# Rotating start places for the two parts of each weight chunk in a float32r decoder trunk

## The chip, the cores and the metric

The kernel runs on one core of one Trainium2 chip. The metric is the device time of one execution in microseconds (us). TensorE is called PE here, its loads of the stationary operand PEld, VectorE DVE, ScalarE ACT, GpSimd POOL and SyncE SP.

## The reference

Two residual layers over 256 tokens of 2048 features, float32, and one final norm. The first layer mixes tokens with a gated MLP, the second with an attention that forgets; each is followed by a feed-forward part with a short causal convolution. Cut to its products:

```python
def chunked_gmlp(xn, w_in, v_norm, w_s, b_s, w_out):
    z = jax.nn.gelu(xn @ w_in, approximate=False)          # 2048 -> 4096
...
    return gated @ w_out                                   # 2048 -> 2048

def conv_ffn(xn, w_up, conv_w, conv_b, w_down):
    h = xn @ w_up                                          # 2048 -> 11264
...
    return (jax.nn.silu(gate) * val) @ w_down              # 5632 -> 2048
...
for l in range(DEPTH):
    if l < N_A:
        h = h + chunked_gmlp(rmsnorm(h, a_norm[l]), ...)
    else:
        h = h + forgetting_attention(rmsnorm(h, b_norm[j]), w_qg, ..., k_sh, v_sh, c_sh)
    h = h + conv_ffn(rmsnorm(h, f_norm[l]), f_w_up[l], ...)
    if l == N_A - 1:
        k_sh, v_sh, c_sh = fox_shared_kv(h, kv_norm, w_kvf, b_f, k_norm)
return rmsnorm(h, final_norm)
```

Nearly all of the arithmetic is the products with the big weight matrices. Every weight is used once.

## The kernel before

All weights flow through one stream of 786 chunks (class `Stream`). A chunk is 128 partitions of up to 1024 float32 values. For each chunk three steps are issued: `_load` brings it from memory into `raw` (by SP's DMA queue, six chunks ahead), `_split` makes two parts of it (three chunks ahead), and `mult` multiplies. The split is one ACT instruction (L82), which writes `whi`, the weight rounded to the matmul's float32r format, and one DVE instruction (L83), which writes `wlo`, the rest that the rounding left. `raw`, `whi` and `wlo` have four buffers each, which are used in turn.

The activations are held in two parts too, side by side: columns 0 to 255 of a feature tile are the rounded part, columns 256 to 511 its rest. They lie in `X1` (shown as X), `mlp_X`, `att_X` or `ffn_H`, by the stage.

There are two forms of product, and in them the weight parts play opposite roles:

- `feat_block` (656 chunks: both FFNs, the MLP's u and output, the gate and the attention's output). The weights are stationary, and PE loads 128x128 pieces of `whi` and `wlo` in turn. For each piece of `whi` it streams 512 columns of activations past, and for the piece of `wlo` 256 columns (only the rounded part). A chunk is eight such pairs of matmuls. The last product of a block, and that alone, has the two the other way round.
- `tok_block` (128 chunks: the MLP's v, the attention's q, k and v). The activations are stationary, and 512 columns of `whi`, `wlo` and again `whi` stream past: twelve matmuls of 512 columns to a chunk. The blocks for the MLP's v and for q use X, those for k and v use att_X.

One more chunk makes the forget gates, with 16 columns of weights at a time. Sums stay in PSUM for a block's whole length; then ACT and DVE take them out while PE goes on with the next block's `ps` buffer (there are three).

The order of the instructions on each engine is that in which the program is written, since the schedule is manual. Where a tile lies in a partition's memory follows from the order and size of the pools: constants with `X1`, then the pool of `raw`, `whi` and `wlo`, then small tiles, then the phase's own tiles (`mlp_X`, `att_X`, `ffn_H` and the rest). Each tile begins on a multiple of 32 bytes. In the built program all eight buffers of `whi` and `wlo` begin 32 bytes past a multiple of 64, and so does `X1` (byte 36,192); `mlp_X`, `att_X` and `ffn_H` begin at byte 129,152, which is a multiple of 64. Inside a tile, every operand of a product begins a multiple of 512 bytes from the tile's start (64 bytes in the forget chunk).

Of the kernel before, what the change touches and what calls it, by code (L numbers as in the profile page):

```python
# [10 lines left out]
F32 = mybir.dt.float32  # L11
F32R = mybir.dt.float32r
# [5 lines left out]
P = 128  # L18
# [4 lines left out]
KF = FFN // P  # L23
NH = 16
CHUNK = 1024
EPS = 1e-6
SCALE = 128 ** -0.5
AHEAD = 3
LOADS = 6
NEG = -3e38  # L30

# Columns of the packed per-partition constants.
C_ANORM, C_KVNORM, C_BNORM, C_FNORM, C_FINAL, C_AVNORM = 0, 16, 32, 48, 80, 96
C_KNORM, C_QNORM, C_BF = 112, 113, 114
C_CONVW = 115
# [2 lines left out]


class Stream:  # L40
    """Weights that stream past: each chunk is loaded, split into two exact parts and multiplied."""

    def __init__(self, nc, pool):
        self.nc, self.pool = nc, pool
# [28 lines left out]
    def _split(self, i):  # L73
        if self.items[i][3]:
            self.items[i][3]()
        raw = self.raw.pop(i, None)
        if raw is None:
            return
        n = raw.shape[1]
        hi = self.pool.tile([P, CHUNK], F32R, name="whi", tag="whi")  # L80
        lo = self.pool.tile([P, CHUNK], F32R, name="wlo", tag="wlo")
        self.nc.scalar.activation(hi[:, :n], raw, AF.Copy)  # L82
        self.nc.vector.tensor_tensor(lo[:, :n], raw, hi[:, :n].bitcast(F32), op=OP.subtract)  # L83
        self.parts[i] = (hi, lo)
# [18 lines left out]


class Phase:
    """Tiles that live as long as one phase; the memory passes to the next phase."""

    def __init__(self, tc):
        self.tc, self.ctx, self.pool, self.name = tc, None, None, None
# [23 lines left out]
def build(ctx, tc, d, out):  # L133
# [26 lines left out]
    def column(i):  # L160
        return col[:, i:i + 1]

    # ------------------------------------------------------------ products
    def mm(o, a, b, start, stop):
        nc.tensor.matmul(o, a, b, start=start, stop=stop, skip_group_check=True)  # L165

    def feat_block(src, x, K, done):
        """[256 features, tokens], weights stationary; the result is the sum of both halves of columns."""
        box = {}
        n = K // 4  # L170
        for c in range(n):
            def mult(hi, lo, c=c):
                if c == 0:
                    box["ps"] = main_ps()
                ps, xx = box["ps"], x()
                for j in range(4):
                    kt = 4 * c + j
                    for m in range(2):
                        w = slice(j * 256 + m * P, j * 256 + (m + 1) * P)
                        if kt < K - 1:  # L180
                            mm(ps[:, m, :], hi[:, w], xx[:, kt, :], kt == 0, False)
                            mm(ps[:, m, :T], lo[:, w], xx[:, kt, :T], False, False)
                        else:
                            mm(ps[:, m, :T], lo[:, w], xx[:, kt, :T], False, False)
                            mm(ps[:, m, :], hi[:, w], xx[:, kt, :], False, True)
                if c == n - 1:
                    s.start(done(ps))
            s.chunk(src[c], mult)

    def tok_block(src, x, done, load=None, prep=None):  # L190
        """[tokens, 512 features], activations stationary; load(c), prep(c): what comes ahead of chunk c."""
        box = {}
        cuts = [(c, 0, 2) for c in range(8)]
        if prep:
            cuts[:1] = [(0, 0, 1), (0, 1, 1)]
        for c, j0, nj in cuts:
            def mult(hi, lo, c=c, j0=j0, nj=nj):
                kt0 = 2 * c + j0
                if kt0 == 0:
                    box["ps"] = main_ps()  # L200
                ps, xx = box["ps"], x()
                for j in range(nj):
                    kt = kt0 + j
                    w = slice(j * 512, (j + 1) * 512)
                    for tb in range(2):
                        a = xx[:, kt, tb * P:(tb + 1) * P]
                        b = xx[:, kt, T + tb * P:T + (tb + 1) * P]
                        mm(ps[:, tb, :], a, hi[:, w], kt == 0, False)
                        mm(ps[:, tb, :], a, lo[:, w], False, False)
                        mm(ps[:, tb, :], b, hi[:, w], False, kt == KD - 1)  # L210
                if kt0 + nj == KD:
                    s.start(done(ps))
            s.chunk(src[c][:, j0 * 512:(j0 + nj) * 512], mult,
                    load and c and (lambda c=c: load(c)), prep and c and (lambda c=c: prep(c)))

    # ------------------------------------------------------------ helpers
    def prep(dst, kt, gain):
        """dst[kt] = the two parts of h[kt] * gain."""
        g = column(gain + kt)
        nc.scalar.activation(dst[:, kt, :T], h[:, kt, :], AF.Copy, scale=g)  # L220
        nc.vector.scalar_tensor_tensor(dst[:, kt, T:], h[:, kt, :], g, dst[:, kt, :T].bitcast(F32),  # L221
                                       op0=OP.mult, op1=OP.subtract)
# [3 lines left out]
        nc.vector.tensor_tensor(dst[..., T:], src, dst[..., :T].bitcast(F32), op=OP.subtract)  # L226

    def rsqrt(y, v, n):
        """y = v ** -0.5: a guess from halving the exponent, then Newton's steps."""
        t = small.tile([P, n], F32, name="rs_t", tag=f"rs_t{n}", bufs=2)  # L230
        nc.vector.tensor_scalar(y.bitcast(I32), v.bitcast(I32), -0.5, 1597463007.0, op0=OP.mult, op1=OP.add)
        for _ in range(3):
            nc.vector.scalar_tensor_tensor(t, y, -0.5, y, op0=OP.mult, op1=OP.mult)
            nc.vector.tensor_tensor(t, t, v, op=OP.mult)
            nc.vector.scalar_tensor_tensor(y, t, 1.5, y, op0=OP.add, op1=OP.mult)

    def token_sums(rest=None):
        """rcol = (sum over features of acc, and rest, / D + eps) ** -0.5."""
        mp = misc_ps()
        parts = [acc] + ([] if rest is None else [rest[:, 0, :], rest[:, 1, :]])  # L240
        for tb in range(2):
            for i, a in enumerate(parts):
                nc.tensor.matmul(mp[:, tb:tb + 1], a[:, tb * P:(tb + 1) * P], ones[:, :1],  # L243
                                 start=i == 0, stop=i == len(parts) - 1)
        v = small.tile([P, 2], F32, name="ts_v", tag="ts_v", bufs=2)
        nc.vector.tensor_scalar(v, mp[:, :2], 1.0 / D, EPS, op0=OP.mult, op1=OP.add)
        rsqrt(rcol, v, 2)

    def token_rows():
        """rcol's values along the columns, the same on every partition."""  # L250
        mp = misc_ps()
        for tb in range(2):
            nc.tensor.transpose(mp[:, tb * P:(tb + 1) * P], rcol[:, tb:tb + 1].to_broadcast([P, P]), ident)
        return mp
# [15 lines left out]
                eng.tensor_tensor(acc, acc, sq[:, i, :], op=OP.add)  # L270

    def scaled_sum(ps, a):
        """a = (ps[.., :T] + ps[.., T:]) * rB."""
        t = small.tile([P, 2, T], F32, name="half", tag="half", bufs=2)
        nc.scalar.activation(t, ps[:, :, T:], AF.Copy)  # L275
        nc.vector.tensor_tensor(a, ps[:, :, :T], t, op=OP.add)  # L276
        nc.vector.tensor_tensor(a, a, rB[:, None, :].to_broadcast([P, 2, T]), op=OP.mult)  # L277

    def residual(p, gain):
        """Add a pair of feature tiles to h; then the next norm's operand and sum of squares."""  # L280
        def done(ps):
            hh = h[:, 2 * p:2 * p + 2, :]
            nc.vector.tensor_tensor(hh, hh, ps[:, :, :T], op=OP.add)
# [7 lines left out]
        return done  # L291

    def final(p, gain):
        """As residual, but the norm's result is the output."""
        def done(ps):
            kts = (2 * p, 2 * p + 1)
            sq = small.tile([P, 2, T], F32, name="sq", tag="sq", bufs=2)
# [18 lines left out]
            yield  # L316
        return done

    # ------------------------------------------------------------ input
    def load_input(c):  # L320
        nc.sync.dma_start(h[:, 2 * c:2 * c + 2, :], d["xT"][:, 2 * c:2 * c + 2, :])

# [13 lines left out]
        yield  # L336
        nc.scalar.activation(rB, token_rows()[:, :T], AF.Copy)

    # ------------------------------------------------------------ gated MLP
    def mlp_kept():  # L340
        ph.open("mlp")
        return (ph.keep("X2", [P, KD, 2 * T], F32R), ph.keep("vt", [P, 2, D]), ph.keep("wT", [P, NH, P]),
# [55 lines left out]
            two_parts(X2[:, 2 * p:2 * p + 2, :], u)  # L398
        return done

    # ------------------------------------------------------------ convolved FFN
    def ffn_h():
        ph.open(f"ffn{state['layer']}")
        return ph.keep("H", [P, KF, 2 * T], F32R)
# [28 lines left out]
        for p in range(8):  # L433
            feat_block(d[f"down{l}"][11 * p:11 * p + 11], ffn_h, KF, done(p))

    # ------------------------------------------------------------ attention
    def att(key):
        ph.open("att")
        shape = {"X2": [P, KD, 2 * T], "q": [P, NH, T], "k": [P, NH, T], "v": [P, 2, D],
# [8 lines left out]
            yield  # L448

    def head_norm(key, blk, gain):  # L450
        """q or k of four heads: normed per head, then features on the partitions."""
        def done(ps):
            dst = att(key)
            for tb in range(2):
# [44 lines left out]
        s.start(forget_sums(ps))  # L499

    def forget_sums(ps):
        """c = cumulative sum of log sigmoid(f), log1p as 2 atanh(y / (2 + y)) in its series."""
        t = [ph.temp("big", [P, 512], bufs=6) for _ in range(2)]
        z, m, y, q = (t[i][:NH, j * T:(j + 1) * T] for i in range(2) for j in range(2))
        nc.scalar.activation(z, ps[:NH, 0, T:], AF.Copy)
# [77 lines left out]
        state["done"] += 1  # L583

    def heads():
        """Starts a head at every second step."""
        n = 0
        while n < NH:
            if state["heads"]:
# [17 lines left out]
            state["gates"] += 1  # L607
        return done

    # ------------------------------------------------------------ the stream  # L610
    state = {"layer": 0, "heads": [], "done": 0, "gates": 0}
    cd = dram.tile([NH, T], F32, name="cd")

    nc.scalar.dma_start(col[:, :C_KVNORM], d["col"][:, :C_KVNORM])
    load_input(0)
    nc.gpsimd.memset(ones, 1.0)
    warm = small.tile([P, 2], F32, name="warm")
    nc.scalar.activation(warm, ones, AF.Gelu)
    nc.gpsimd.memset(ident, 1.0)
    nc.gpsimd.affine_select(ident, ident, pattern=[[-1, P]], compare_op=OP.is_equal, fill=0.0,  # L620
                            base=0, channel_multiplier=1)
# [31 lines left out]


def feat_chunks(w, order=None):
    """[K, N] -> chunks [N / 256 * K / 512, 128, 4 * 256]; order: the 128-wide tiles of the columns."""
    K, N = w.shape
    a = w.reshape(K // 512, 4, P, N // P, P)
    if order is not None:
# [3 lines left out]


def tok_chunks(w):
    """[K, N] -> chunks [N / 512 * K / 256, 128, 2 * 512]."""
    K, N = w.shape
    a = w.reshape(K // 256, 2, P, N // 512, 512)
    return np.ascontiguousarray(a.transpose(3, 0, 2, 1, 4)).reshape(-1, P, CHUNK)
# [43 lines left out]
```

## Time and profile before

| what | value |
|---|---|
| median of 3 runs | 2284.31 us (2284.15 to 2284.43) |
| span of the profiled execution, first to last instruction | 2282.4 us |
| outside that span (median less span) | 1.9 us |
| PE busy, share of the span | 99% |
| mean granted TensorE clock | 0.997 |
| memory traffic | 184 GB/s over the span |

The profiled execution is known by its span. The runs were timed without a profile, and their median lies 1.9 us above that span, which is what a run has around its instructions. A matmul's recorded duration is longer than its share of the time, since matmuls overlap; how fast PE goes is read from the starts, or from a stretch of the chain divided by the number of matmuls in it.

### The profile page before, as it was taken

Reading aid. Unit: us, or ns where it says so; the run is one execution under the profiler, and the core shown is the slowest. Engines: PE = TensorE matmul, PEld = TensorE weight load, DVE = VectorE, ACT = ScalarE, POOL = GpSimd, SP = SyncE. Lnnn points to the kernel's source line nnn. Section 1 sums busy time; section 2 is a strip of 40 time slices with the busy share of each in tenths; the row PEclk is TensorE's granted clock in tenths of the full one; section 3 lists DMA queues with packets and bytes.
Section 4 is the critical chain, followed back from the end, with each engine's and each line's share of the span. In section 5 each row is a group of like instructions: output and inputs, shape, how many; then the busy total and the mean of one; then the engine's idle time right before and its main releaser. Section 6 shows DMA issues by size and latency. Waiting matters only on the chain.

```text
span 2282.4 us, 32221 instructions
## 1 busy us (share of the span) xinstructions
PE 2262.3 (99%) x12440; PEld 1945.8 (85%) x12440; DVE 1541.6 (68%) x2212; ACT 1189.5 (52%) x1622; POOL 34.5 (2%) x56
## 2 busy tenths in 40 slices
PE   8999999999999999999999999999999999999997
PEld 6888888888888888888788888888888888888886
DVE  6566677777777755557776567677777777764554
ACT  6544455555555544445444666455555555553442
POOL 3000000000000000000000110000000000000000
PEclk9999999999999999999999999999999999999998
DMA  7555555555555555555555555555555555556553
GB/s 281 188 184 170 189 187 187 189 186 186 186 189 186 185 180 189 192 186 175 168 188 184 167 163 181 180 186 190 187 186 189 188 186 186 187 181 193 185 185 120
DMA packets 116442, 422.11 MB, mean 185 GB/s; under 512 B 13232, under 2 KB 13376, under 8 KB 116032
## 3 DMA queue, kind: packets, MB, share of 16 engines
q1 hardware_dynamic: 115344, 417.93, 56.1%
q0 software_dynamic: 768, 2.10, 0.3%
q8 instruction: 97, 1.59, 0.3%
q14 instruction: 57, 0.47, 0.1%
q10 hardware_dynamic: 176, 0.02, 0.0%
HBM read 417.88 MB, written 2.11 MB: 184 GB/s over the span
## 4 chain that ended last, share of the span: by engine, by line
PE 98%; DVE 1%; ACT 0%; DMA 0%; issue 0%; SPq 0%; DVEq 0%
PE ps L165 96%; PE mp L387 0%; PE mp L471 0%; PE mp L557 0%; PE mp L572 0%; DMA h<-xT 0%; DVE wlo L83 0%; DVE X L221 0%; PE mp L580 0%; PE mp L581 0%; PE mp L556 0%; PE mp L579 0%; DVE h L313 0%; ACT X L220 0%; PE mp L243 0%
## 5 line engine op out<-in xcount | busy, mean ns | idle before, releaser
L83 DVE TENSOR_TENSOR wlo<-raw,whi 128x1024 fp32r<-128x1024 f32 (+1 forms) x786 | 957.0, 1223 | 499.4 <-ACT whi L82 479.9
L165 PE MATMUL ps<-X,whi 128*128 128x512 f32 x3328 | 1171.8, 398 | 0.0
L82 ACT ACTIVATE whi<-raw 128x1024 fp32r<-128x1024 f32 (+1 forms) x786 | 824.3, 1053 | 585.6 <-PE ps L165 543.1
L165 PE MATMUL ps<-X,wlo 128*128 128x256 f32 x3328 | 918.3, 281 | 0.0
L165 PEld LDWEIGHTS ps<-X,whi 128*128 128x128 f32 x3328 | 619.3, 188 | 143.0
L165 PEld LDWEIGHTS ps<-X,wlo 128*128 128x128 f32 x3328 | 624.8, 188 | 9.1
L165 PE MATMUL ps<-ffn_H,whi 128*128 128x512 f32 x1408 | 496.3, 397 | 0.0
L165 PE MATMUL ps<-ffn_H,wlo 128*128 128x256 f32 x1408 | 393.5, 281 | 0.0
L165 PEld LDWEIGHTS ps<-ffn_H,whi 128*128 128x128 f32 x1408 | 263.3, 188 | 63.8
L165 PEld LDWEIGHTS ps<-ffn_H,wlo 128*128 128x128 f32 x1408 | 265.4, 188 | 1.5
L165 PE MATMUL ps<-whi,X 128*128 128x512 f32 x512 | 163.6, 397 | 5.9 <-ACT whi L82 5.9
L165 PE MATMUL ps<-whi,att_X 128*128 128x512 f32 x512 | 169.4, 402 | 0.0
L421 DVE SCALAR_TENSOR_TENSOR ffn_c<-ffn_a,col,ffn_c 128x255 f32<-128x255 f32 x352 | 161.9, 481 | 6.3
L275 ACT ACTIVATE half<-ps 128x512 f32<-128x512 f32 x104 | 62.3, 599 | 184.0 <-PE ps L165 184.0
L276 DVE TENSOR_TENSOR ffn_a<-ps,half 128x512 f32<-128x512 f32 x88 | 61.0, 693 | 111.2 <-ACT half L275 111.2
L417 ACT ACTIVATE ffn_c<-ffn_a,col 128x256 f32<-128x256 f32 x176 | 96.5, 596 | 47.6 <-DVE ffn_a L277 47.6
L165 PEld LDWEIGHTS ps<-whi,X 128*128 128x128 f32 x512 | 97.1, 190 | 26.6 <-ACT whi L82 5.9
L165 PEld LDWEIGHTS ps<-whi,att_X 128*128 128x128 f32 x512 | 96.0, 188 | 22.2
L165 PE MATMUL ps<-wlo,X 128*128 128x512 f32 x256 | 101.1, 395 | 1.2 <-DVE wlo L83 1.2
L165 PE MATMUL ps<-wlo,att_X 128*128 128x512 f32 x256 | 101.0, 395 | 0.0
L165 PE MATMUL ps<-att_X,whi 128*128 128x512 f32 (+1 forms) x272 | 95.5, 396 | 0.0
L165 PE MATMUL ps<-mlp_X,whi 128*128 128x512 f32 x256 | 90.0, 397 | 0.0
(140 smaller groups left out, 1264.7 us busy)
## 6 DMA issues: line engine op xcount, KB each, us to landing
raw<-up SPq DMA_DIRECT2D x352, 512.0 KB, 3.4
raw<-down SPq DMA_DIRECT2D x176, 512.0 KB, 4.3
raw<-a_in_u SPq DMA_DIRECT2D x32, 512.0 KB, 3.4
raw<-a_out SPq DMA_DIRECT2D x32, 512.0 KB, 3.3
raw<-b_q SPq DMA_DIRECT2D x32, 512.0 KB, 4.2
raw<-kvf_k SPq DMA_DIRECT2D x32, 512.0 KB, 4.3
raw<-kvf_v SPq DMA_DIRECT2D x32, 512.0 KB, 3.4
raw<-b_g SPq DMA_DIRECT2D x32, 512.0 KB, 3.3
```

The lines of the kernel that those rows point to most:

```text
L82: self.nc.scalar.activation(hi[:, :n], raw, AF.Copy)
L83: self.nc.vector.tensor_tensor(lo[:, :n], raw, hi[:, :n].bitcast(F32), op=OP.subtract)
L165: nc.tensor.matmul(o, a, b, start=start, stop=stop, skip_group_check=True)
L275: nc.scalar.activation(t, ps[:, :, T:], AF.Copy)
L276: nc.vector.tensor_tensor(a, ps[:, :, :T], t, op=OP.add)
L417: nc.scalar.activation(c[:, m, :], a[:, m, :], AF.Identity, scale=w[2], bias=column(C_CONVB + l * 2 * KF + f))
L421: nc.vector.scalar_tensor_tensor(c[:, m, n:], a[:, m, :T - n], w[k], c[:, m, n:], op0=OP.mult, op1=OP.add)
```

## The change

`whi` and `wlo` get 12 more columns (48 bytes). Chunk number i puts its `whi` part 16 bytes times (i mod 4) into its buffer, and its `wlo` part 16 bytes times (i div 4 mod 4). Sixteen chunks so go through all sixteen pairs of places. The number i also counts the few items of the stream that have no weights.

```diff
 CHUNK = 1024
+PAD = 12
...
         n = raw.shape[1]
-        hi = self.pool.tile([P, CHUNK], F32R, name="whi", tag="whi")
-        lo = self.pool.tile([P, CHUNK], F32R, name="wlo", tag="wlo")
+        hi = self.pool.tile([P, CHUNK + PAD], F32R, name="whi", tag="whi")
+        lo = self.pool.tile([P, CHUNK + PAD], F32R, name="wlo", tag="wlo")
+        hi = hi[:, 4 * (i % 4):][:, :CHUNK]
+        lo = lo[:, 4 * (i // 4 % 4):][:, :CHUNK]
         self.nc.scalar.activation(hi[:, :n], raw, AF.Copy)
         self.nc.vector.tensor_tensor(lo[:, :n], raw, hi[:, :n].bitcast(F32), op=OP.subtract)
...
     nc.gpsimd.memset(ones, 1.0)
-    warm = small.tile([P, 2], F32, name="warm")
-    nc.scalar.activation(warm, ones, AF.Gelu)
+    nc.scalar.activation(rcol, ones, AF.Gelu)
```

The second piece lets an early ACT instruction, whose result nobody reads, write into `rcol` instead of a tile of its own; that tile goes. Comments go as well. The instructions and their order are the same on every engine, but for the name of that one output.

Two things follow for the places. A buffer of 4144 bytes takes 4160, so all eight buffers still begin 32 bytes past a multiple of 64, and the parts come to lie 32, 48, 0 or 16 bytes past one. And what lies behind the pool moves up by 8 x 64 bytes less the 32 of the dropped tile, 480 bytes: `mlp_X`, `att_X` and `ffn_H` begin at 129,632, which is 32 bytes past a multiple of 64, as `X1` does before and after.

## Rows read from the trace of the kernel before

**Rows 1.** The page: span, and busy time of each engine

```profile
span 2282.4 us, 32221 instructions
PE 2262.3 (99%) x12440; PEld 1945.8 (85%) x12440; DVE 1541.6 (68%) x2212; ACT 1189.5 (52%) x1622; POOL 34.5 (2%) x56
```

**Rows 2.** The page's chain that ended last, shares of the span by engine

```profile
PE 98%; DVE 1%; ACT 0%; DMA 0%; issue 0%; SPq 0%; DVEq 0%
```

**Rows 3.** That chain in order of time, stretches of feat_block: start, length, count

```profile
199.42 93.10 PE ps L165 x528
298.84 739.72 PE ps L165 x4184
...
1379.66 146.76 PE ps L165 x832
1532.74 734.23 PE ps L165 x4160
```

**Rows 4.** The same view, stretches of tok_block

```profile
1061.67 8.26 PE ps L165 x36
1107.44 8.26 PE ps L165 x36
1206.21 8.40 PE ps L165 x36
1215.04 14.00 PE ps L165 x60
```

**Rows 5.** Groups by shape on PE, window 1107.44 to 1115.6 us: count, busy us, mean ns

```profile
L165 PE MATMUL ps<-whi,X 128*128 128x512 f32 x24 | 7.7, 394 | 0.0
L165 PE MATMUL ps<-wlo,X 128*128 128x512 f32 x12 | 4.7, 394 | 0.0
```

**Rows 6.** Groups by shape on PE, window 1206.21 to 1214.5 us

```profile
L165 PE MATMUL ps<-whi,att_X 128*128 128x512 f32 x24 | 7.8, 398 | 0.0
L165 PE MATMUL ps<-wlo,att_X 128*128 128x512 f32 x12 | 4.7, 395 | 0.0
```

**Rows 7.** Timeline of PE in an up-projection: start, duration (us), tile

```profile
599.72 0.40 PE L165 MATMUL ps<-X,whi 128*128 128x512 f32 x1
...
602.20 0.40 PE L165 MATMUL ps<-X,whi 128*128 128x512 f32 x1
```

**Rows 8.** Timeline of PE in a down-projection

```profile
900.48 0.40 PE L165 MATMUL ps<-ffn_H,whi 128*128 128x512 f32 x1
...
900.84 0.39 PE L165 MATMUL ps<-ffn_H,whi 128*128 128x512 f32 x1
...
901.18 0.40 PE L165 MATMUL ps<-ffn_H,whi 128*128 128x512 f32 x1
...
901.54 0.39 PE L165 MATMUL ps<-ffn_H,whi 128*128 128x512 f32 x1
...
901.89 0.40 PE L165 MATMUL ps<-ffn_H,whi 128*128 128x512 f32 x1
...
902.25 0.39 PE L165 MATMUL ps<-ffn_H,whi 128*128 128x512 f32 x1
...
902.60 0.40 PE L165 MATMUL ps<-ffn_H,whi 128*128 128x512 f32 x1
```

**Rows 9.** Who waited for whom: us in total, times, longest

```profile
ACT whi L82 <- PE ps L165: 543.1, 390, 2.2
DVE wlo L83 <- ACT whi L82: 479.9, 379, 4.7
```

**Rows 10.** Line 165: what PE waited for, us and times

```profile
  ACT whi L82: 11.8, 2
  DVE wlo L83: 4.8, 9
```

**Rows 11.** Groups by shape on DVE and ACT: count, busy us, mean ns, idle before

```profile
L83 DVE TENSOR_TENSOR wlo<-raw,whi 128x1024 fp32r<-128x1024 f32 x783 | 955.3, 1225 | 498.6 <-ACT whi L82 479.1 <-PE ps L165 6.2
L421 DVE SCALAR_TENSOR_TENSOR ffn_c<-ffn_a,col,ffn_c 128x254 f32<-128x254 f32 x176 | 85.0, 483 | 6.3
L392 DVE SCALAR_TENSOR_TENSOR mlp_mixed<-mp,col,mlp_bB 128x256 f32<-128x256 f32 x16 | 7.0, 479 | 3.7 <-PE mp L387 3.7
L82 ACT ACTIVATE whi<-raw 128x1024 fp32r<-128x1024 f32 x783 | 822.7, 1055 | 585.6 <-PE ps L165 543.1 <-ACT whi L82 19.8 <-DMA raw<-a_in_v 7.4
```

**Rows 12.** Busy time by stretch, 300 to 1030 us: PE, PEld, DVE, ACT, POOL, clock, DMA

```profile
300.00:1030.00 730.00, 730.00 (x4138) 634.58 (x4137) 497.81 (x652) 382.13 (x500) 0.00 (x0) 1.00 0.58 187
```

## Prediction

> **What bounds the kernel now.** I began with the busy shares and the chain that ended last: PE is busy for 99% of the span, and 98% of the chain is PE's [rows 1, 2]. So nothing counts here but what changes the pace of PE, or makes it wait. The reader is to see next that PE does not wait for the parts: in the whole execution it waited 11.8 us for `whi` and 4.8 us for `wlo`, 11 times in all [rows 10]. Those who make the parts wait for PE: ACT's rounding stood 543.1 us because PE still held the buffer, and DVE's subtraction 479.9 us behind ACT [rows 9]. In the middle of the run the clock granted to PE is 1.00, its upper level of 2.4 GHz, and the DMA engines are busy 58% [rows 12].
>
> Then I read PE's pace. In `feat_block` the chain has stretches in which matmul follows matmul. 739.72 us for 4184 matmuls is 2092 pairs of 353.6 ns; 734.23 us for 4160 gives 353.0, 146.76 us for 832 gives 352.8 and 93.10 us for 528 gives 352.7 [rows 3]. A pair streams 768 columns, which at one column per cycle of 2.4 GHz are 320 ns. So each pair has 33 ns that are not columns, about 16.5 per matmul. With 5248 pairs (656 chunks of eight) that is 5248 x 33 ns = 173 us, and it is the only thing on which a start address could act here.
>
> In `tok_block` 36 matmuls of 512 columns take 8.26 us with X as the stationary operand, 229.4 ns each, and 8.40 us with att_X, 233.3 ns each (60 in 14.00 us say the same) [rows 4 to 6]. 512 columns are 213.3 ns, so the surplus is 16.1 ns in one case and 20.0 in the other. Shape, weights' buffers, clock and program are the same. The difference that I find is the place: X begins 32 bytes past a multiple of 64, as the streamed parts do, and att_X on such a multiple. So places do seem to matter to PE, by 3.9 ns per matmul of 512 columns.
>
> In `feat_block` a similar contrast is there, and it comes to nothing. With X streaming, seven pairs take from 599.72 to 602.20 us, 354 ns each [rows 7]. With ffn_H streaming, which begins on a multiple of 64 while the stationary parts lie 32 past one, the pairs alternate: 0.36, 0.34, 0.36, 0.35, 0.36, 0.35 us [rows 8]. The slow ones are 360 ns, the fast ones 1.04 / 3 = 347, and the mean is 353.5, as with X. Another relative place changed the pattern and not the pace.
>
> **The change part by part.** No instruction is added, removed or moved. Three things change.
>
> *The early ACT instruction that writes rcol.* It runs before anything else reads or writes rcol. It stays one instruction on two columns, under the first loads, and costs what it did: nothing more, covered or not.
>
> *ACT and DVE write and read at other bytes.* The nearest row for an operand off the 32-byte grid is the convolution's instruction on 254 columns, which starts 8 bytes in: 483 ns, against 479 for an aligned one on 256 columns, on DVE [rows 11]. Were it 1% of each split, DVE's 1225 ns and ACT's 1055 would grow by some 12 and 11 ns. DVE is busy 497.81 of 730 us there [rows 12], so of the 2.83 us that a chunk has (eight pairs) about 0.9 is free; the split also runs three chunks ahead. It is hidden many times over. Without the cover it would be 786 x 12 ns = 9 us.
>
> *PE's operands lie elsewhere.* This is the whole question, with two terms.
>
> (a) `tok_block`. The streamed parts go from one place to four, and att_X comes to where X lies. For parts at the same place as the stationary tile I have 229.4 ns, for 32 bytes apart 233.3; for 16 and 48 bytes apart there is no row. Bounds: below 229.4 and above 233.3 by these rows. I take the middle for the two unseen ones, so the mean over four places is 231.35 in all stages. X's 768 matmuls lose 768 x 1.95 ns = 1.5 us, att_X's 768 gain 1.5 us. Sum: 0. With the bounds it is 3 us either way.
>
> (b) `feat_block`. The streamed tiles all lie 32 past a multiple of 64 now; the stationary parts at four places each. For parts 0 and 32 bytes from the streamed tile the mean pair is 353.5 in both cases, the two relative places that the trace has. For 16 and 48 bytes no row exists. The nearest bounds are the fast and the slow pair of the alternation: 347 and 360, 6.5 ns either way, or 34 us if all 5248 pairs went there. As the step from 0 to 32 bytes left the mean where it was, I take 353.5 for the rest too, and 0 us. For the range I let half of the pairs reach one end or the other, 17 us.
>
> The sum is then 2282.4 us of the profiled span, plus 1.9 us around it by the median of the runs shown, plus 0: 2284.3, say **2284 us**.
>
> The Trainium skill, in "SBUF — State Buffer", section "Specifications (TRN2)", says that the memory is read in lines of 16 bytes and that crossing to a new line costs something. Places in steps of 16 bytes never add a line, so by it every part costs what it costs now and the sum is the present time exactly, 2284.3 us. The 3.9 ns of the tok stages, where both places are on 16-byte lines too, do not fit a rule that stops there.
>
> **The rivals.**
>
> *The odd places are slow.* All tiles lie on multiples of 32 bytes now, and the change puts half of the parts at 16 or 48 bytes past a multiple of 64, off that grid. For it: the tok stages show that a place can cost 3.9 ns per matmul. Against it: where the streamed tile and the parts lay 32 bytes apart in `feat_block`, it cost nothing. Price: the same 3.9 ns for the half of all matmuls that touch an odd part, 6032 x 3.9 = 23.5 us, giving 2308 us. It decides from 4.6 us on, that is from 0.38 ns as a mean over the 12,064 matmuls, or 0.8 ns for each odd one.
>
> *The present place is a bad one.* Where X streams, both parts and X lie at the same place, and what lies at one place could collide with itself. For it: in the alternation of ffn_H every second pair is 6.5 ns faster. Against it: the pair next to it pays that back, and in `tok_block` the same place is the faster one. Price: a fast pair in a quarter to a half of the combinations without paying back, 1312 to 2624 pairs x 6.5 ns = 9 to 17 us, so 2275 to 2267 us, 2273 in the middle.
>
> *Places mean nothing to PE.* Then the tok difference has another cause, the attention's own tiles perhaps, and the time stays at 2284.3 us. For it: equal means in `feat_block`. Against it: 229.4 and 233.3, repeated stretch by stretch, and the alternation that is there with ffn_H and not with X. Beside it, the Trainium skill, "TensorE: Matmul & The Clock Gate", section "Step-by-step: what each phase is for", says that streaming and loading weights have read ports of their own, so that loading takes nothing from a running matmul; then no pair of places could beat another, and the time is again 2284.3 us.
>
> **How the numbers follow.** A measurement of this kernel can tell about 0.2%, 4.6 us, from no change. My forecast, that the places balance, has 0.26, and that they mean nothing 0.12; both end within 0.2%, together 0.38. The odd places slow: 0.36. The present place bad: 0.26. I put slower above faster because one of the sides has a mechanism that touches half of all matmuls, while the gain needs a fast pair that is not paid back. The range reaches from 2265 us (half of the pairs fast, 17 us, and 2 us of the 3 in the tok stages) to 2308 us (the slow rival's price), and should leave out 2 in 10. Where nothing or little comes of it, the forecast's own range is 2280 to 2289.
>
> **What would show it.** In the trace after, the chain's long stretch from about 299 us on should hold 353 to 354 ns per pair, with pairs that differ from chunk to chunk in a pattern of sixteen chunks: this shows that places act and balance. If every chunk takes the same time, places mean nothing. If chunks with an odd place stand out by more than 6 ns (eight pairs, 0.8 ns each), the first rival holds; if chunks whose parts lie away from X are shorter, the second. The tok stages with X and with att_X should come to the same 231 ns. DVE's and ACT's splits should stay within 15 ns of 1225 and 1055, and PE's waits for them near the present 17 us. Wrong would be the forecast above all if an odd place costs PE more than a relative place of 32 bytes does, since no row of this trace has an operand of a product there.

## The result, and the profile after

The changed kernel takes 2269.43 us (median of 4 runs, 2269.36 to 2270.42) where the kernel before takes 2284.23 in the same session. The ratio is 0.9936, with a 95% interval of 0.9922 to 0.9950: 14.8 us faster. Its profiled execution has a span of 2268.7 us, against 2282.4. The time lies in the forecast range, and well below the forecast itself. It is the time that the rival gave which called the present place a bad one.

The page's head and the long stretches of `feat_block` in the chain that ended last (start, length, count), of the kernel after, answer to [rows 1, 3]:

```profile
span 2268.7 us, 32221 instructions
PE 2248.0 (99%) x12440; PEld 1941.2 (86%) x12440; DVE 1541.3 (68%) x2212; ACT 1194.0 (53%) x1622; POOL 34.6 (2%) x56
```

```profile
200.50 92.45 PE ps L168 x528
...
299.21 733.78 PE ps L168 x4184
...
1374.11 145.38 PE ps L168 x832
...
1525.76 727.11 PE ps L168 x4160
```

The same 9704 matmuls, 4852 pairs, took 1713.81 us before [rows 3] and take 1698.72 now. That is 353.2 ns per pair before and 350.1 after, 15.1 us in all, a little more than the span lost. No wait went: PE does the same instructions at a quicker pace. The clock granted is the same too, as the stretch that answers to [rows 12] shows (PE, PEld, DVE, ACT, POOL, clock, DMA share, GB/s); PE gets through 4168 matmuls in the 730 us, where it was 4138:

```profile
300.00:1030.00 730.00, 730.00 (x4168) 638.05 (x4167) 499.83 (x656) 385.55 (x504) 0.00 (x0) 1.00 0.57 188
```

In `tok_block` a little is given back. Stretches of the chain in q (X stationary, the first two) and in k (att_X, the last two), against [rows 4]:

```profile
1056.36 8.36 PE ps L168 x36
...
1102.73 8.36 PE ps L168 x36
...
1201.41 8.34 PE ps L168 x36
1210.19 13.98 PE ps L168 x60
```

In the stretches of 36 a matmul went from 229.4 to 232.2 ns with X, and from 233.3 to 231.7 with att_X (8.34 / 36); in that of 60 it is 233.0. The four stages together tell it better. The mean distance between starts, where matmul follows matmul, went from 229.1 to 232.5 ns with X (v of the MLP and q) and from 233.1 to 232.0 with att_X (k and v).

The splits did not change. DVE's and ACT's groups (count, busy us, mean ns, idle before), and PE's waits for them, against [rows 10, 11]:

```profile
L86 DVE TENSOR_TENSOR wlo<-raw,whi 128x1024 fp32r<-128x1024 f32 x783 | 955.3, 1225 | 487.5 <-ACT whi L85 472.1 <-PE ps L168 6.1
...
L85 ACT ACTIVATE whi<-raw 128x1024 fp32r<-128x1024 f32 x783 | 823.1, 1056 | 569.7 <-PE ps L168 532.8 <-ACT whi L85 18.7 <-DMA raw<-a_in_v 7.4
```

```profile
  ACT whi L85: 12.2, 2
  DVE wlo L86: 6.1, 11
```

The time of a chunk now goes up and down in a pattern of sixteen chunks. In the first up-projection, behind its first sixteen chunks, they take from 2784 to 2827 ns, and all 144 chunks that can be compared with the one sixteen later agree with it within 2 ns. So the pace of a chunk does hang on the places, and the mean over the places is better than what all chunks had before.

### The profile page after: what moved, and what is told of

Same layout as the page of the kernel before. It is cut to its first block, busy times and chain, and to the rows that moved or that the text cites. A ratio compares the mean times of both kernels' runs of the same rounds, so it can differ in the third digit from the quotient of the medians.

```text
span 2268.7 us, 32221 instructions
## 1 busy us (share of the span) xinstructions
PE 2248.0 (99%) x12440; PEld 1941.2 (86%) x12440; DVE 1541.3 (68%) x2212; ACT 1194.0 (53%) x1622; POOL 34.6 (2%) x56
## 4 chain that ended last, share of the span: by engine, by line
PE 98%; DVE 1%; ACT 0%; DMA 0%; issue 0%; SPq 0%; DVEq 0%
PE ps L168 96%; PE mp L390 0%; PE mp L474 0%; PE mp L560 0%; DMA h<-xT 0%; PE mp L575 0%; DVE X L224 0%; DVE wlo L86 0%; PE mp L583 0%; PE mp L584 0%; PE mp L559 0%; PE mp L582 0%; DVE h L316 0%; PE mp L246 0%; ACT whi L85 0%
```

## The experiments

Two theories stood against each other. **P1**: each relation of places has a pace of its own; the kernel before sits in a slow one everywhere, and turning averages over slow and fast. **U**: whatever stays in place settles at the slow pace, and turning helps because it keeps throwing the streams out of step. A third thing had to be told apart, since the change does it too: **M**, the move of mlp_X, att_X and ffn_H by 480 bytes.

**Longer buffers alone** (`e1_longer_only`).

```diff
-        hi = hi[:, 4 * (i % 4):][:, :CHUNK]
-        lo = lo[:, 4 * (i // 4 % 4):][:, :CHUNK]
+        hi = hi[:, 4 * (0):][:, :CHUNK]
+        lo = lo[:, 4 * (0):][:, :CHUNK]
```

> The buffers are longer, so mlp_X, att_X and ffn_H move by 480 bytes as in the change, but every part begins at its buffer's start. Theory P (the turning places of the parts make the gain, 14.8 us): pairs stay at 353 to 354 ns in every feat_block stage, the tok stages with att_X come down from 233.3 to 229.4 ns per matmul (3 us), so 2281 us, 2279 to 2285. Rival M (moving the other tiles makes the gain): about 2269 us with the ffn_H stages faster.

Measured: 2277.92 us, ratio 0.9972 (0.9962 to 0.9982). Both numbers were missed: 6.5 us came without any turning. The stage to look at is the up-projection with X, where, counted within 64 bytes, nothing moved. Yet its chunks took four different times in turn, 2814, 2833, 2803 and 2810 ns. A block of that stage has four chunks too, and the kernel before has four times there as well, but from 2818 to 2827 only. The down-projection, whose blocks have eleven chunks, leaves just the buffers: 2830, 2817, 2792 and 2821 ns, again and again, where before all chunks inside a block took 2826 or 2827. Buffers now begin 4160 bytes apart, which is no multiple of 128 or 256, so the four lie differently within 256 bytes. The frame of 64 bytes, in which the prediction thought, is too small. Buffers that differ by 128 bytes, the first and the third, are not alike either (2830 and 2792).

**The tiles moved alone** (`e5_tiles_moved`).

```diff
-    warm = small.tile([P, 2], F32, name="warm")
-    nc.scalar.activation(warm, ones, AF.Gelu)
+    warm = small.tile([P, 128], F32, name="warm")
+    nc.scalar.activation(warm[:, :2], ones, AF.Gelu)
```

> The kernel before, with a longer unused tile alone: mlp_X, att_X and ffn_H begin 480 bytes later, whi and wlo stay as they were. Theory B (of the 6.5 us that longer buffers alone brought, the feat_block part comes from the buffers, which then lie 4160 bytes apart, no multiple of 256, and not from the moved tiles): pairs stay at 353.3 ns with ffn_H, now in the even pattern of X; tok stages with att_X come to 229 ns; 2281 us, 2280 to 2283. Rival M (the moved tiles bring it): 2278 us.

Measured: 2282.07 us, ratio 0.9989 (0.9980 to 0.9999). As theory B said: k and v, with att_X where X lies, run at X's pace (229.4 ns per matmul), and `feat_block` did not change. The chain in this kernel, first `feat_block`, then k:

```profile
299.61 739.76 PE ps L165 x4184
```

```profile
1205.91 8.26 PE ps L165 x36
1214.61 13.76 PE ps L165 x60
```

So M is worth 2.2 us, and of the 6.5 us above the other 4.3 come from the uneven buffers. By the starts of the matmuls in `e1_longer_only` these brought 6.6 us in `feat_block` and took about as much in `tok_block` as M gave there.

**One part turns** (`e3_hi_turns`, `e4_lo_turns`).

```diff
         hi = hi[:, 4 * (i % 4):][:, :CHUNK]
-        lo = lo[:, 4 * (i // 4 % 4):][:, :CHUNK]
+        lo = lo[:, 4 * (0):][:, :CHUNK]
```

The second has `whi` at 0 and `wlo` turning.

> whi turns through its four places, wlo stays at its buffer's start. If the gain is the sum of what each part brings: about half, 2274 to 2278 us. If only the relation of the two parts counts: all of it, 2268 to 2271 us. If whi does not matter: 2281 us, as with the longer buffers alone.

> wlo turns through its four places, each for four chunks, whi stays at its buffer's start. If the gain is the sum of what each part brings: about half, 2274 to 2278 us. If only the relation of the two parts counts: all of it, 2268 to 2271 us. If wlo does not matter: 2281 us.

Measured: 2273.32 us (ratio 0.9952, 0.9937 to 0.9966) with `whi` turning, 2269.23 (0.9934, 0.9917 to 0.9950) with `wlo`. The first lies just below the band for half, the second in the band for all. Against the longer buffers alone, `whi` brings 4.6 us, `wlo` 8.7 and both together 8.5. The parts do not add up, and these two alone did not decide between the theories.

**Buffers that lie evenly** (`e6_even_buffers`, `e7_even_turning`). To keep the four buffers alike within 256 bytes they got 256 bytes more each; the room was made with one buffer of `raw` fewer.

```diff
-LOADS = 6
+LOADS = 5
+PAD = 64
...
+        hi = hi[:, 4 * (0):][:, :CHUNK]
+        lo = lo[:, 4 * (0):][:, :CHUNK]
```

In the second kernel the places turn as in the change. In both, ffn_H, mlp_X and att_X lie 2048 bytes lower than before, which within 256 bytes is their old place, so M is not in them.

> Buffers 256 bytes longer (4352 bytes apart, a multiple of 256) with every part at its start; to make room there is one buffer of raw fewer and loads run five chunks ahead. Theory B (longer buffers help only because the four then lie at different places within 256 bytes): no gain, 2283 to 2286 us, pairs at 353.3 ns. Rival: the gain comes with any longer buffer, 2278 us.

> As the even buffers, with the places turning as in the change: only 16 places of 0 to 48 bytes, no help from uneven buffers. If the turning of the parts by itself is enough: 2268 to 2272 us. If a good share came from the uneven buffers: 2273 to 2279 us.

Measured: 2288.59 us (ratio 1.0018, 1.0009 to 1.0028) and 2274.50 us (0.9956, 0.9939 to 0.9973). The first is 4.3 us above before, more than expected, but not in `feat_block`: its longest stretch is that of before to the hundredth [rows 3].

```profile
298.78 739.72 PE ps L168 x4184
```

By the starts of its chunks this kernel loses 0.5 us in k and 3.9 us in the fifth and sixth chunk of the attention's v stage, at about 1238 to 1244 us, and nothing after that. The trace shows what happened there. ACT stood 3.60 us for a load of `raw`; DVE's part of the head norm, which stands in line behind the split, came late; and PE stood 2.16 us before it could transpose. Timeline of ACT, then of PE, then busy time by stretch (PE, PEld, DVE, ACT, POOL, clock, DMA share, GB/s):

```profile
1234.23 1.06 ACT L85 ACTIVATE whi<-raw 128x1024 fp32r<-128x1024 f32 x1 [3.60 <-DMA raw<-kvf_v]
```

```profile
1240.46 1.08 PE L474 MATMUL mp<-ident,att_big 128*128 128x128 f32 x4 [2.16 <-DVE att_big L468]
```

```profile
1240.40:1244.30 3.90, 3.84 (x12) 3.27 (x13) 3.23 (x3) 1.63 (x2) 0.00 (x0) 0.57 0.50 153
```

After that stand the granted clock is 0.57 for 3.9 us, near its lower level of 1.2 GHz; matmuls there start up to 430 ns apart in place of 233, and that makes up the rest. That the load was late because it was issued one chunk less ahead fits, and was not tried apart. So longer buffers bring nothing by themselves. From the first to the second it is 14.1 us, nearly all of the change's 14.8: turning does it without uneven buffers. The 2274.50 us lie in the band that was expected for the opposite, only because these 4.3 us were not foreseen; its trace has the same loss in the same chunks.

**Each pair of places held** (`e2_held`, `e8_even_held`). The decisive question is what a place does that stays. In both kernels each pair of places is kept for eleven chunks in the projections, in the first with the change's buffers, in the second with the even ones.

```diff
-        hi = hi[:, 4 * (i % 4):][:, :CHUNK]
-        lo = lo[:, 4 * (i // 4 % 4):][:, :CHUNK]
+        k = self.count
+        self.count += 1
+        p = held(k)
+        hi = hi[:, 4 * (p % 4):][:, :CHUNK]
+        lo = lo[:, 4 * (p // 4):][:, :CHUNK]
```

`held` gives the pairs in turn in the first up-projection and backwards in the second; each down-projection has eight of them.

> Each pair of places is held for 11 chunks in a row (up and down projections) or 4 (elsewhere), in all sixteen pairs. Theory P1 (each pair of places has a pace of its own, and turning them averages it): held chunks differ from pair to pair by 20 to 50 ns, the same pair gives the same time in both up-projections, the mean over the sixteen is 2800 ns per chunk as with turning, and the time is 2267 to 2273 us. Rival U (a place that stays lets the streams settle into a slow pattern, and each change of place throws them out of it for a few matmuls): held chunks go back to about 2827 ns whatever the pair, only the first chunk after a change is short, and the time is 2280 to 2284 us.

> As the even buffers, each of the sixteen pairs of places held for 11 chunks in a row (88 pairs of matmuls with nothing that changes but the chunk). Theory P1 (each pair of places has a pace of its own): after the first chunk the eleven chunks of a pair of places agree within 5 ns, both up-projections give the same number for the same pair, and the sixteen differ, some at 2827 ns and some at 2770 to 2800. Theory U (whatever is held settles at 353.3 ns a pair, in another pattern): all sixteen end at 2822 to 2828 ns, and the time is near 2283 us.

Measured: 2269.33 us and 2277.82 us, one run each. With the change's buffers a held pair still gave chunk times in cycles of four, since the buffers differ. With even buffers the answer is plain, above all in the down-projections. Timeline of PE in `e8_even_held` (start, duration, tile): the first matmul of a chunk and the one eight chunks later, for `whi` and `wlo` 0 and 0, then 16 and 0, then 32 and 0 bytes in:

```profile
784.79 0.39 PE L196 MATMUL ps<-ffn_H,whi 128*128 128x512 f32 x1
...
807.41 0.39 PE L196 MATMUL ps<-ffn_H,whi 128*128 128x512 f32 x1
```

```profile
815.86 0.39 PE L196 MATMUL ps<-ffn_H,whi 128*128 128x512 f32 x1
...
838.25 0.39 PE L196 MATMUL ps<-ffn_H,whi 128*128 128x512 f32 x1
```

```profile
846.62 0.40 PE L196 MATMUL ps<-ffn_H,whi 128*128 128x512 f32 x1
...
868.81 0.40 PE L196 MATMUL ps<-ffn_H,whi 128*128 128x512 f32 x1
```

Eight chunks take 22.62, 22.39 and 22.19 us: 2827, 2799 and 2774 ns each. The mean settled time of a chunk (from the starts of its matmuls; the sixth to tenth chunk in the up-projections, the third to tenth in the down-projections):

| `whi`, `wlo` bytes in | up, first | up, second | down |
|---|---|---|---|
| 0, 0 | 2824 | 2824 | 2827 |
| 16, 0 | 2822 | 2824 | 2800 |
| 32, 0 | 2784 | 2786 | 2773 |
| 48, 0 | 2825 | 2825 | 2827 |
| 0, 16 | 2798 | 2798 | 2773 |
| 16, 16 | 2827 | 2827 | 2773 |
| 32, 16 | 2806 | 2807 | 2805 |
| 48, 16 | 2793 | 2775 | 2800 |
| 0, 32 | 2823 | 2823 | 2773 |
| 16, 32 | 2803 | 2803 | 2773 |
| 32, 32 | 2775 | 2776 | 2827 |
| 48, 32 | 2799 | 2799 | 2827 |
| 0, 48 | 2783 | 2786 | 2791 |
| 16, 48 | 2801 | 2803 | 2773 |
| 32, 48 | 2805 | 2804 | 2795 |
| 48, 48 | 2825 | 2825 | 2827 |

Fifteen of sixteen pairs come back within 3 ns in the second up-projection, in the opposite order. Their means are 2806, 2805 and 2798 ns, where the kernel before has 2826.7 settled. So U falls: places that stay settle, and by no means all at the slow pace. The number that P1 named for agreement, 5 ns from the second chunk on, held in fifteen of sixteen pairs of the down-projections, the last chunk left out, which ends a block. In the up-projections, where every fourth chunk ends a block and the order of the two parts is turned round, it held in 3 of 32; there it is the mean that comes back. One pair did not obey: with 48 and 16 the first up-projection stayed at 2816 to 2827 ns for seven chunks and then went to 2770 to 2781, the second was at 2770 to 2784 all along. Two paces are open to that pair, and how it came to be in the one is not settled.

The table holds one more test. In the built program ffn_H lies 32 bytes past X, within 256. So a part that lies 32 bytes further on has to ffn_H the distance that it had to X, and four pairs can be compared: 0 and 0, 16 and 0, 0 and 16, 16 and 16 in the up columns with 32 and 32, 48 and 32, 32 and 48, 48 and 48 in the down column. That is 2824 and 2827, 2822 to 2824 and 2827, 2798 and 2795, 2827 and 2827. The same distance gives the same time within 5 ns, whichever tile streams.

**A version from the table** (`e9_one_place`, `e10_parts_32_on`). If P1 holds, nothing need turn: all parts 32 bytes on, and the tiles of the stages put where X lies within 256 bytes.

```diff
+    gap = const.tile([P, 8], F32, name="gap")
...
+    nc.gpsimd.memset(gap, 0.0)
-    warm = small.tile([P, 2], F32, name="warm")
-    nc.scalar.activation(warm, ones, AF.Gelu)
+    warm = small.tile([P, 56], F32, name="warm")
+    nc.scalar.activation(warm[:, :2], ones, AF.Gelu)
```

The second kernel has the gap without the longer `warm`, so that ffn_H, mlp_X and att_X move along with the parts.

> The kernel before with all buffers 32 bytes further on and mlp_X, att_X and ffn_H moved so that they lie like X within 256 bytes; nothing turns. Theory P1 (each relation of places settles at its own pace; the held run gave 2773 to 2778 ns per chunk for both parts 32 bytes on against X, and 2822 to 2828 as it was): 656 feat_block chunks gain about 49 ns each, 32 us; tok_block with X loses 53 ns on 64 chunks, 3.4 us; 2253 to 2259 us. Rival U (variety is what helps, one place for all settles at the slow pace): 2282 to 2288 us.

> The same shift of the parts by 32 bytes, but everything behind the pool only moves along by 32 bytes, so the relation to ffn_H, mlp_X and att_X is what it was in the kernel before. Theory R (the relation of stationary and streamed places counts, not where they are): the 416 feat_block chunks with X gain as in the one-place kernel (20 us), the 240 others stay at 2825 ns, tok_block with X loses 3.4 us; 2265 to 2270 us. Rival (the parts' own place counts): all 656 chunks gain, 2253 to 2259 us.

Measured: **2255.65 us** (ratio 0.9875, 0.9860 to 0.9890) and 2267.18 us (0.9925, 0.9910 to 0.9940). Both are inside the bands of P1 and R. The first is 28.7 us faster than before and 13.8 faster than the change. Its long stretches in the chain, against [rows 3]:

```profile
199.46 91.58 PE ps L166 x528
...
297.26 727.01 PE ps L166 x4184
...
1366.66 144.30 PE ps L166 x832
...
1517.18 721.41 PE ps L166 x4160
```

They add up to 1684.30 us, 347.1 ns per pair. In `tok_block` this kernel loses, as was expected: 233.3 ns per matmul with X, where it was 229.1. In the timeline the slow seven pairs of [rows 7] (2.48 us) have become eight in 2.78 us, 347.5 ns each:

```profile
599.57 0.39 PE L166 MATMUL ps<-X,whi 128*128 128x512 f32 x1
...
602.35 0.39 PE L166 MATMUL ps<-X,whi 128*128 128x512 f32 x1
```

The second kernel shows that it is the relation that counts. Timeline of PE, a chunk's first matmul and that of the eighth chunk after it, in the first up-projection and in the first down-projection:

```profile
412.29 0.39 PE L166 MATMUL ps<-X,whi 128*128 128x512 f32 x1
...
434.49 0.39 PE L166 MATMUL ps<-X,whi 128*128 128x512 f32 x1
```

```profile
902.92 0.39 PE L166 MATMUL ps<-ffn_H,whi 128*128 128x512 f32 x1
...
925.54 0.39 PE L166 MATMUL ps<-ffn_H,whi 128*128 128x512 f32 x1
```

Eight chunks take 22.20 us with X and 22.62 with ffn_H, the parts at the same bytes. Over the whole stages the means are 2775 ns, as in the first kernel, and 2825, where the first kernel has 2774. Between the two kernels the parts and X lie alike; the stages' own tiles, ffn_H, mlp_X and att_X among them, lie 192 bytes apart.

**Steps of 4 bytes** (`e11_steps_of_4`).

```diff
-        hi = hi[:, 4 * (i % 4):][:, :CHUNK]
-        lo = lo[:, 4 * (i // 4 % 4):][:, :CHUNK]
+        hi = hi[:, i % 4:][:, :CHUNK]
+        lo = lo[:, i // 4 % 4:][:, :CHUNK]
```

> The change with steps of 4 bytes in place of 16: parts begin 0, 4, 8 or 12 bytes into their buffers, off the lines of 16 bytes in three of four cases. If a part that begins off a 16-byte line costs an extra line: slower than the longer buffers alone (2278 us), 2280 us or more. If a shift of 4 bytes already changes the relation of the streams: 2268 to 2273 us as with steps of 16. If places within 16 bytes are one to PE: 2278 us, as with the longer buffers alone.

Measured: 2278.12 us, ratio 0.9973 (0.9962 to 0.9983), the time of the longer buffers alone. That is the third answer by the time, and the trace does not support it. Chunk by chunk the two kernels differ: in the first up-projection 3 of 174 comparable chunks agree within 2 ns. And the tok stages are slower than there, 8.46 us for 36 matmuls in q where the longer buffers alone have 8.32:

```profile
1060.74 8.46 PE ps L168 x36
```

```profile
1060.09 8.32 PE ps L168 x36
```

So steps of 4 bytes act too; that the total is the same is a balance: against the longer buffers alone `tok_block` loses 2.6 us and `feat_block` gains 2.3. In `tok_block` with X a matmul takes 231.1 ns with the longer buffers alone, 233.1 here and 232.5 with steps of 16 bytes. Turning by 16 bytes costs a like amount, so this run does not tell a price of leaving the 16-byte lines from a price of turning.

**Turning in feat_block alone** (`e12_turn_in_feat`).

```diff
+        turn = 33 <= k < 361 or k >= 458
-        hi = hi[:, 4 * (i % 4):][:, :CHUNK]
-        lo = lo[:, 4 * (i // 4 % 4):][:, :CHUNK]
+        hi = hi[:, 4 * (i % 4) * turn:][:, :CHUNK]
+        lo = lo[:, 4 * (i // 4 % 4) * turn:][:, :CHUNK]
```

> The change with places turning in feat_block alone; in tok_block parts stay at their buffers' starts. Theory: the tok stages with X get back the 2.8 us that turning cost them, the feat_block stages keep their 16 us; 2265 to 2268 us. Rival (tok's loss came from the longer buffers and not from turning): 2269 us.

Measured: 2268.03 us, ratio 0.9930 (0.9915 to 0.9945), between the two expectations and on the edge of the first. q went back to 8.30 us for 36 matmuls, 230.6 ns, and not to 229.4. Over all matmuls with X it is 231.1 ns, as with the longer buffers alone, so of the 3.3 ns that the change cost there, turning has 1.3 and the uneven buffers have 2.0.

## Why the prediction was right in its range and wrong in its centre

**What bounds the kernel** was right, and everything came from it: PE's pace per pair, with the 33 ns per pair that are not columns as the only thing to act on. Of the 33 ns, the change took 3.1 and the one-place kernel 6.1.

**The ACT and DVE terms** were right: 1056 and 1225 ns after, PE's waits 18.3 us in place of 16.6 (12.2 and 6.1).

**Term (a)**, the tok stages, had the signs right. X's matmuls lost 3.3 ns where 1.95 was the estimate, att_X's gained 1.1 where it was 1.95. The sum is 768 x 2.2 ns = 1.7 us lost in place of 0.

**Term (b)** is the step that failed: "As the step from 0 to 32 bytes left the mean where it was, I take 353.5 for the rest too, and 0 us." Two relations of places with one mean were taken for all of them. The sixteen held pairs show that 353.3 (2827 ns per chunk) is the slowest settled pace in the table, that five or six of sixteen pairs have it or nearly so and that others go down to 346.7. Chance had put the kernel before into this slow pace twice, with X and with ffn_H. The measured term is 3.1 ns x 5248 = 16 us of gain. Of the sign that it named for places that act and balance, the pattern of sixteen chunks came, and the 353 to 354 ns did not: the long stretch holds 350.8 (733.78 us for 2092 pairs).

What misled was the alternation of [rows 8]. The fast pair there was read as paid back by the slow one, which is true of that place; it was taken to speak against a place that is fast all the time, and such places exist. The bounds that it gave, 347 to 360, were good: 347.1 is what the one-place kernel runs at. And the range was made by letting half of the pairs go to the fast end, 17 us, where 16 were measured. That half was a choice which no row supported; that it came so close is luck.

**The rivals.** "The present place is a bad one" was the case, at 2269.4 us within the 2275 to 2267 at which it was priced (their middle is 2271, not the 2273 that the prediction gives), for the reason that fast pairs are not paid back. Its picture of like places colliding is not shown: parts 32 bytes off the streamed tile's place within 64 bytes are fast with X in the one-place kernel and slow with ffn_H in the kernel before, and with X the pair 16 and 16 is as slow as 0 and 0. With places held, the same distance gave `feat_block` the same time wherever two stages could be compared, but no rule was found by which a distance is fast or slow. "The odd places are slow" is refuted: 0 and 16, 16 and 32, 16 and 48 are among the fastest with ffn_H. "Places mean nothing" is refuted by the period of sixteen chunks.

On the last of these the prediction named the Trainium skill, "TensorE: Matmul & The Clock Gate", section "Step-by-step: what each phase is for": loading weights takes no read bandwidth from a running matmul. The runs differ from what was drawn from it, that no pair of places could beat another: with the same instructions the pair goes from 353.2 to 347.1 ns when only the relation of the loaded and the streamed operand changes. On the sum it named the Trainium skill, "SBUF — State Buffer", section "Specifications (TRN2)", with lines of 16 bytes. What was drawn from it, that places in steps of 16 bytes all cost the same, does not agree with the traces either: such steps move a held chunk from 2827 to 2800 or 2773 ns.

**The frame of 64 bytes** was wrong as well. In `e10_parts_32_on` X and ffn_H both lie 32 bytes, within 64, from the parts; the one gives 2775 ns and the other 2825. They differ by 64 bytes in their place. The traces point to a frame of 256 bytes: in `e1_longer_only` buffers that differ by 128 bytes within 256 take different times, and in `e6_even_buffers`, with buffers 4352 bytes apart (17 x 256), `feat_block` runs as before, to the hundredth. No run varied the frame by itself.

## What to carry to other kernels

When PE is busy without a gap and its matmuls still take longer than their columns, read the starts in the timeline: a surplus that is the same in every pair can hang on where the stationary and the streamed operand lie relative to one another. Two stages with the same mean say nothing of the places that were not tried. One kernel that holds each place for some ten chunks tells nearly all of them at once (one pair in sixteen showed two paces here), and one place that is fast for most of the work beats turning: 2255.65 us against 2269.43. It need not be the best for every form of product: the one-place kernel is the fastest in `feat_block` and among the slowest in `tok_block`.

## What the runs showed of the hardware

Settled chunks of `feat_block` take 2826.7, 2800 or 2773.3 ns in thirteen of the sixteen pairs held in the down-projections, and something between in the other three: steps of 26.7 ns per chunk of sixteen matmuls, 3.33 ns per pair. In `tok_block`, with one place for all parts, a matmul takes 229.1 ns with X before and 233.3 with the parts 32 bytes further on. Patterns within a chunk differ at the same level: 235 and 118 ns all along with X before, 229, 117, 240, 121 with ffn_H, both 706.7 ns for two pairs. The loads and the splits are not needed for it: in the kernel before, the last two chunks that can be timed begin after the last split has ended and take 2826 and 2827 ns, as the others of their block. What in PE or the memory makes the steps, and why one pair of places has two paces, is open.
